# Value products of a head with its high and low columns in one stationary operand, in an encoder trunk on one core

## The chip, the cores and the metric

The kernel runs on one core of a Trainium2 chip. The metric is the device time of one execution in microseconds (us). It was run three times before the change: 2228.54, 2228.63 and 2228.89 us, median 2228.63.

## The reference

A trunk of two layers for 256 tokens of width 2048, in float32. Each layer norms its input, projects it to 4608 columns, and hands these to three groups: a gated convolution of width 31 with a layer norm, attention with 16 heads of 64, and a pooling group. Their results are normed, scaled, concatenated, projected back and added to the input; a gated feed-forward part of 5632 hidden columns follows. The attention mixes three dilated windows; for 256 tokens this comes to one softmax with a mask that adds a logarithm for keys seen by several windows:

```python
wgt = jnp.exp(m_all - jnp.max(m_all, axis=0, keepdims=True))
num = jnp.sum(wgt[..., None] * o_all, axis=0)
den = jnp.sum(wgt * s_all, axis=0)
out = num / den[..., None]
```

## The kernel before, in words

**Weights.** Every large product is x times a weight matrix, 512 output columns at a time (a `Job`). Activations and weights are split into a high and a low part of the type fp32r, and three products are summed: high x high, high x low, low x high (lines 139 to 141). A job is cut into groups of two blocks of 128 rows; a group is one DMA of 512 KB on SP's queue (line 90), a ScalarE copy that rounds to the high part (line 104) and a VectorE subtraction for the low part (line 113).

**Steps.** The order of the work is written out by hand. The main loop (line 876) goes through one group per step `s`: it first copies and splits the weights of the group three steps ahead (`pump`), then emits six matmuls for the first 128 tokens (`t` = 0) with the group of this step, then six for the other 128 tokens (`t` = 1) with the group four steps back, and last it calls `run_tasks`. When a job's last group is done for a `t`, its `done` function is called right behind the six matmuls. So a step is twelve matmuls and what the tasks add, and each engine works through its own instructions in this order. The tile framework adds the semaphores.

**Tasks.** A task is a generator. Each `yield n` means "go on n steps later" (1 without a number); `spawn(task, n)` starts it n steps later, and one that is due runs in the same call. Tasks run in the order of their start. `tr_free` (line 171) lets one of them per step take the tile for transposes; the transposes of q and k reserve theirs three steps after their projection.

**Attention.** The 16 heads are two halves of eight (called 0.0 to 0.7 and 1.0 to 1.7 in what follows; the code's names are `hf` and `h`). For each half q, k and v are projected in this order, two halves one after the other; each is a job of eight groups. In layer 0 the value projection of half 0 is done (`v_done`, line 521) at step 51 for `t` = 1, the one of half 1 at step 75, the k projection of half 1 at step 71. `v_last` starts the heads of half 0 one step later, every second step from 52 on; `k_last` (line 645) starts those of half 1 five steps after k, two in three steps, at 72, 73, 75, 76 and so on. The second layer has the same steps from its own start.

`head_task` (line 534) is one head: scores on TensorE (line 543, rows `r0` of 64, six matmuls), mask and maximum on VectorE (line 548), and the negated maximum on GpSimd; one step later the exponentials on ScalarE (line 556); one step later 1/denominator and normalisation on VectorE (lines 562 and 564); two steps later four transposes on TensorE (line 571), the high part on ScalarE (line 575) and the low part on VectorE (line 576); two steps later the value products (line 584). These take all 128 value columns of a pair of heads as stationary operand, so each head computes 64 rows that nobody reads: v high x p high, v high x p low, v low x p high for two blocks of keys, six in all, into `po[:, h % 2]`. `po` is one accumulator bank for the pair. After the odd head, in the same step, ScalarE scales the two row halves into the high part (line 600) and squares them (line 604), VectorE makes the low part (line 606), and GpSimd adds the squares (line 611). Two steps after the last pair `ssb` sums the squares over the rows (line 616) for the norm of the attention group.

Beside the first half's heads, the convolution runs on VectorE (line 383, three or four operations a step to step 57), then its layer norm (lines 395 to 412, with three operations of 512 columns per `t` at steps 61 and 65), and the transposes for the output product. From step 72 the output projection runs; its finished chunks are copied by ScalarE (`ac_done`, line 678), for `t` = 0 at steps 75, 79, 83 and 87 and for `t` = 1 four steps later.

**Buffers.** `s2` has six buffers of 512 columns for `pt` (the probabilities), `pT` (two per head), `sq` and others. `trp` has two accumulator banks, `scp` (scores) and `pop` (value results) one each.

Of the kernel before, what the change touches and what calls it, by code (L numbers as in the profile page):

```python
# [7 lines left out]
F32 = mybir.dt.float32  # L8
F32R = mybir.dt.float32r
AF = mybir.ActivationFunctionType  # L10
ALU = mybir.AluOpType
AX = mybir.AxisListType

P = 128
S = 256
NT = S // P
# [6 lines left out]
HD = 64  # L23
ROT = 16
NHH = HALF_B // HD
# [4 lines left out]
NB = 512  # L30
# [11 lines left out]
def hybrid_encoder_kernel(  # L42
# [6 lines left out]
    nc = tc.nc  # L49
# [4 lines left out]
    s4 = ctx.enter_context(tc.tile_pool(name="s4", bufs=23))  # L54
    s2 = ctx.enter_context(tc.tile_pool(name="s2", bufs=6))
# [96 lines left out]
    def spawn(gen, delay=0):  # L152
        tasks.append([clock["step"] + delay, gen])
# [17 lines left out]
    def tr_free():  # L171

        k = clock["step"]
        if used.get(k):
            return False
        used[k] = True
        return True
# [59 lines left out]
    rs_in = {}  # L237
# [82 lines left out]
    def mixer_jobs(l):  # L320
        st = {}
# [199 lines left out]
        def v_done(hf):  # L521
            def done(t, ps):
                if t == 0:
                    st["v", hf] = [
                        s4.tile([P, NT, NB], F32R, tag="s4", name="v") for _ in range(2)
                    ]
                hi, lo = (a[:, t] for a in st["v", hf])
                nc.scalar.activation(hi, ps, AF.Copy, scale=rs_in[t])
                nc.vector.scalar_tensor_tensor(
                    lo, ps, rs_in[t], hi.bitcast(F32), ALU.mult, ALU.subtract  # L530
                )
            return done

        def head_task(hf, h):
            qT, kT, v = st["qT", hf], st["kT", hf], st["v", hf]
            pr, r0 = h // 2, (h % 2) * HD
            sc = scp.tile([P, NT, S], F32, tag="sc", name="sc")
            pt = s2.tile([P, NT, S], F32, tag="s2", name="pt")
            mx = sm.tile([P, NT], F32, tag="mx", name="mx")
            den = sm.tile([P, NT], F32, tag="den", name="den")  # L540
            for t in range(NT):
                for i, (a, b) in enumerate(((0, 0), (0, 1), (1, 0))):
                    nc.tensor.matmul(  # L543
                        sc[:, t], qT[a][r0 : r0 + HD, pr, t * P : (t + 1) * P],
                        kT[b][r0 : r0 + HD, pr], start=i == 0, stop=i == 2,
                    )
            for t in range(NT):
                nc.vector.tensor_tensor_reduce(
                    pt[:, t], sc[:, t], mask[:, (1 - t) * P : (1 - t) * P + S], 1.0, -3.0e38, ALU.add, ALU.max,
                    accum_out=mx[:, t : t + 1],  # L550
                )
            nmx = sm.tile([P, NT], F32, tag="nmx", name="nmx")
            nc.gpsimd.tensor_scalar(nmx, mx, -(HD ** -0.5), None, ALU.mult)
            yield
            for t in range(NT):
                nc.scalar.activation(
                    pt[:, t], pt[:, t], AF.Exp, bias=nmx[:, t : t + 1], scale=HD ** -0.5,
                    accum_out=den[:, t : t + 1],
                )
            yield  # L560
            rden = sm.tile([P, NT], F32, tag="rden", name="rden")
            nc.vector.reciprocal(rden, den)
            for t in range(NT):
                nc.vector.tensor_scalar(pt[:, t], pt[:, t], rden[:, t : t + 1], None, ALU.mult)
            yield 2
            while not tr_free():
                yield
            pst = trp.tile([P, NT, S], F32, tag="tr", name="tr")
            for kt in range(NT):
                for t in range(NT):  # L570
                    nc.tensor.transpose(  # L571
                        pst[:, kt, t * P : (t + 1) * P], pt[:, t, kt * P : (kt + 1) * P], ident
                    )
            pT = [s2.tile([P, NT, S], F32R, tag="s2", name="pT") for _ in range(2)]
            nc.scalar.activation(pT[0], pst, AF.Copy)
            nc.vector.tensor_tensor(pT[1], pst, pT[0].bitcast(F32), ALU.subtract)
            yield 2
            if h % 2 == 0:
                st["po", hf] = pop.tile([P, 2, S], F32, tag="po", name="po")
            po = st["po", hf]  # L580
            n = 0
            for kt in range(NT):
                for a, b in ((0, 0), (0, 1), (1, 0)):
                    nc.tensor.matmul(  # L584
                        po[:, h % 2], v[a][:, kt, pr * P : (pr + 1) * P], pT[b][:, kt],
                        start=n == 0, stop=n == 5,
                    )
                    n += 1
            if h % 2 == 0:
                return  # L590
            if pr == 0:
                yB[hf] = [s4.tile([P, 4, S], F32R, tag="s4", name="yB") for _ in range(2)]
            hi, lo = yB[hf]
            col = G_MX + l * KD + 4 + 4 * hf + pr
            sq = sq_acc
            if (hf, pr) != (0, 0):
                sq = s2.tile([P, S], F32, tag="s2", name="sq")
            rows = [slice(e * HD, (e + 1) * HD) for e in range(2)]
            for e, r in enumerate(rows):
                nc.scalar.activation(  # L600
                    hi[r, pr], po[r, e], AF.Copy, scale=gT[r, col : col + 1]
                )
            for e, r in enumerate(rows):
                nc.scalar.activation(sq[r], po[r, e], AF.Square)
            for e, r in enumerate(rows):
                nc.vector.scalar_tensor_tensor(
                    lo[r, pr], po[r, e], gT[r, col : col + 1], hi[r, pr].bitcast(F32),
                    ALU.mult, ALU.subtract,
                )
            if sq is not sq_acc:  # L610
                nc.gpsimd.tensor_tensor(sq_acc, sq_acc, sq, ALU.add)
            if hf == 1 and pr == 3:
                yield 2
                ssb = scp.tile([P, NT], F32, tag="sc", name="ssb")
                for t in range(NT):
                    nc.tensor.matmul(
                        ssb[:, t : t + 1], sq_acc[:, t * P : (t + 1) * P], ones,
                        start=True, stop=True,
                    )
                ms = sm.tile([P, NT], F32, tag="msb", name="msb")  # L620
                nc.vector.tensor_scalar(ms, ssb, 1.0 / C_B, EPS, ALU.mult, ALU.add)
                rs = sm.tile([P, NT], F32, tag="rsb", name="rsb")
                nc.gpsimd.tensor_tensor(
                    rs, ms, half_neg.to_broadcast([P, NT]), ALU.pow
                )
                for t in range(NT):
                    rs_b[t] = rs[:, t : t + 1]
# [3 lines left out]
        def attn_task(hf, pace):  # L631
            for h in range(NHH):
                spawn(head_task(hf, h))
                yield pace[h % len(pace)]
# [10 lines left out]
        def k_last(hf, pace):  # L645
            base = qk_done("k", hf)

            def done(t, ps):
                base(t, ps)
                if t == NT - 1:  # L650
                    spawn(attn_task(hf, pace), 5)
            return done

        kin = [(k, k) for k in range(KD)]
# [106 lines left out]
    for l in range(DEPTH):  # L761
        jobs, load_layer = mixer_jobs(l)
        a = len(groups)
        add_jobs(jobs)
        seg_info.append((a, len(groups), load_layer, (g_post_mix, l), G_FF + l * KD))
        a = len(groups)
# [31 lines left out]
    for n in range(4):  # L798
        for t in range(NT):
            load_x(t, n)  # L800
            g = 2 * n + t
# [4 lines left out]
    gT = cst.tile([P, NG], F32, name="gT")  # L806
# [9 lines left out]
    rows = {}  # L816
# [48 lines left out]
    col = None  # L865
    for si, (g0, g1, load_layer, post, pre) in enumerate(seg_info):
        n = g1 - g0
# [99 lines left out]
        col = pre  # L967
# [55 lines left out]
```

## Time and profile before

| | |
|---|---|
| Median of three runs | 2228.63 us |
| The profiled execution | 2228.57 us |
| Its span | 2226.8 us |
| TensorE matmul busy | 2208.8 us, 99% of the span, 9860 matmuls |
| VectorE busy | 1287.8 us, 58% |
| ScalarE busy | 1060.3 us, 48% |
| GpSimd busy | 127.9 us, 6% |
| DMA | 400.66 MB, mean 180 GB/s |

The span is the time from the first to the last instruction of the profiled execution; 1.8 us of the execution's time lie around it. In the rows below PE is TensorE (PEld its weight loads), DVE is VectorE, ACT is ScalarE, POOL is GpSimd and SP is SyncE; L584 is line 584 of the kernel, and `out<-in` are the tiles written and read. Matmuls are pipelined, so the time of one is longer than the interval between two. The granted TensorE clock is 1.00 of full speed in both attention stretches.

### The profile page before, as it was taken

Reading aid. Unit: us, or ns where it says so; the run is one execution under the profiler, and the core shown is the slowest. Engines: PE = TensorE matmul, PEld = TensorE weight load, DVE = VectorE, ACT = ScalarE, POOL = GpSimd, SP = SyncE. Lnnn points to the kernel's source line nnn. Section 1 sums busy time; section 2 is a strip of 40 time slices with the busy share of each in tenths; the row PEclk is TensorE's granted clock in tenths of the full one; section 3 lists DMA queues with packets and bytes.
Section 4 is the critical chain, followed back from the end, with each engine's and each line's share of the span. In section 5 each row is a group of like instructions: output and inputs, shape, how many; then the busy total and the mean of one; then the engine's idle time right before and its main releaser. Section 6 shows DMA issues by size and latency. Waiting matters only on the chain.

```text
span 2226.8 us, 26295 instructions
## 1 busy us (share of the span) xinstructions
PE 2208.8 (99%) x9860; PEld 1778.8 (80%) x9860; DVE 1287.8 (58%) x1735; ACT 1060.3 (48%) x1481; POOL 127.9 (6%) x163
## 2 busy tenths in 40 slices
PE   9999999999999999999999999999999999999998
PEld 6887887888888888888778788878888888888886
DVE  5798757455444444455567987574544444444544
ACT  6445756444444443444564566564444444434443
POOL 0001112000000000000210011120000000000002
PEclk9999999999999999999999999999999999999999
DMA  8654355555555655556565544555555555555553
GB/s 268 194 176 136 133 172 178 181 182 186 189 182 187 183 185 186 186 182 204 172 210 177 171 132 149 173 170 180 189 180 189 188 180 183 186 188 181 188 199 123
DMA packets 208608, 400.66 MB, mean 180 GB/s; under 512 B 12730, under 2 KB 16162, under 8 KB 208480
## 3 DMA queue, kind: packets, MB, share of 16 engines
q1 hardware_dynamic: 208448, 398.98, 55.7%
q8 instruction: 77, 1.26, 0.2%
q14 instruction: 51, 0.42, 0.1%
q10 hardware_dynamic: 32, 0.01, 0.0%
HBM read 396.84 MB, written 2.10 MB: 179 GB/s over the span
## 4 chain that ended last, share of the span: by engine, by line
PE 95%; DVE 2%; ACT 2%; issue 1%; DMA 0%; POOL 0%; SPq 0%; DVEq 0%; POOLq 0%; ACTq 0%
PE acc L139 30%; PE acc L140 30%; PE acc L141 30%; PE tr L208 1%; PE sc L543 1%; PE po L584 1%; DVE hl L113 1%; ACT xT L215 1%; PE tr L571 1%; DVE xT L218 0%; ACT junk L202 0%; DMA raw<-in_w_in_dram 0%; DVE x L292 0%; PE tr L512 0%; PE tr L445 0%
## 5 line engine op out<-in xcount | busy, mean ns | idle before, releaser
L113 DVE TENSOR_TENSOR hl<-raw,hl 128x1024 fp32r<-128x1024 f32 x736 | 905.0, 1231 | 767.5 <-ACT hl L104 766.1
L104 ACT ACTIVATE hl<-raw 128x1024 fp32r<-128x1024 f32 x735 | 776.4, 1059 | 761.6 <-PE acc L141 752.7
L139 PE MATMUL acc<-hl,xT 128*128 128x512 f32 x1984 | 796.2, 401 | 1.0 <-DVE hl L102 1.0
L140 PE MATMUL acc<-hl,xT 128*128 128x512 f32 x1984 | 786.7, 397 | 1.4 <-DVE hl L113 1.2
L141 PE MATMUL acc<-hl,xT 128*128 128x512 f32 x1984 | 786.6, 396 | 1.3 <-DVE xT L218 1.3
L141 PEld LDWEIGHTS acc<-hl,xT 128*128 128x128 f32 x1984 | 373.6, 188 | 93.1 <-DVE xT L218 2.6
L139 PEld LDWEIGHTS acc<-hl,xT 128*128 128x128 f32 x1984 | 373.7, 188 | 90.1 <-ACT xT L215 2.0
L140 PEld LDWEIGHTS acc<-hl,xT 128*128 128x128 f32 x1984 | 374.0, 189 | 89.4 <-DVE hl L113 3.3
L139 PE MATMUL acc<-hl,fT 128*128 128x512 f32 x704 | 280.1, 398 | 0.0
L141 PE MATMUL acc<-hl,fT 128*128 128x512 f32 x704 | 279.1, 396 | 0.0
L140 PE MATMUL acc<-hl,fT 128*128 128x512 f32 x704 | 279.0, 396 | 0.0
L141 PEld LDWEIGHTS acc<-hl,fT 128*128 128x128 f32 x704 | 132.6, 188 | 32.3
L140 PEld LDWEIGHTS acc<-hl,fT 128*128 128x128 f32 x704 | 132.7, 188 | 31.8
L139 PEld LDWEIGHTS acc<-hl,fT 128*128 128x128 f32 x704 | 132.6, 188 | 31.7
L272 POOL TENSOR_TENSOR out<-out,gain 128x512 f32<-128x512 f32 x20 | 25.8, 1297 | 1447.4 <-ACT junk L202 1447.4
L383 DVE SCALAR_TENSOR_TENSOR cacc<-hT,cwT,cacc 128x241 f32<-128x241 f32 (+14 forms) x240 | 98.8, 469 | 0.0
L210 ACT ACTIVATE fT<-tr 128x512 fp32r<-128x512 f32 x44 | 26.4, 599 | 96.1 <-PE tr L208 96.1
L211 DVE TENSOR_TENSOR fT<-tr,fT 128x512 fp32r<-128x512 f32 x44 | 30.4, 692 | 68.6 <-ACT fT L210 68.6
L710 ACT ACTIVATE sg<-acc,rsin 128x512 f32<-128x512 f32 x44 | 30.3, 689 | 45.6 <-PE acc L141 45.6
L202 ACT ACTIVATE junk<-out 128x512 bf16<-128x512 f32 x32 | 20.2, 631 | 66.6 <-DVE out L740 42.8
L139 PE MATMUL acc<-hl,yB 128*128 128x512 f32 x128 | 51.1, 399 | 0.0
L140 PE MATMUL acc<-hl,yB 128*128 128x512 f32 x128 | 50.7, 396 | 0.0
(150 smaller groups left out, 1294.5 us busy)
## 6 DMA issues: line engine op xcount, KB each, us to landing
raw<-in_w_gate_dram SPq DMA_DIRECT2D x176, 512.0 KB, 3.5
raw<-in_w_up_dram SPq DMA_DIRECT2D x176, 512.0 KB, 3.5
raw<-in_w_down_dram SPq DMA_DIRECT2D x176, 512.0 KB, 3.6
raw<-in_w_in_dram SPq DMA_DIRECT2D x144, 512.0 KB, 3.6
raw<-in_w_out_dram SPq DMA_DIRECT2D x64, 512.0 KB, 3.5
x<-in_x_dram SPq DMA_DIRECT2D x8, 256.0 KB, 6.9
pm<-in_c_pool_dram SPq DMA_DIRECT2D x4, 512.0 KB, 5.2
gain<-in_g_post_mix_dram SPq DMA_DIRECT2D x4, 512.0 KB, 6.7
```

Source lines behind the costliest of these rows:

```text
L104: nc.scalar.activation(hl[:, 0], raw, AF.Copy)
L113: nc.vector.tensor_tensor(hl[:, 1], raw, hl[:, 0].bitcast(F32), ALU.subtract)
L139: nc.tensor.matmul(ps, xh, hl[:, 0, j], start=first, stop=False)
L140: nc.tensor.matmul(ps, xh, hl[:, 1, j], start=False, stop=False)
L141: nc.tensor.matmul(ps, xl, hl[:, 0, j], start=False, stop=last)
L208: nc.tensor.transpose(pst[:, j], srcs[j], ident)
L210: nc.scalar.activation(dst[:, 0], pst, AF.Copy)
L211: nc.vector.tensor_tensor(dst[:, 1], pst, dst[:, 0].bitcast(F32), ALU.subtract)
L215: nc.scalar.activation(dst[:, 0, j], pst[:, j], AF.Copy, scale=g)
L272: nc.gpsimd.tensor_tensor(o, o, gain, ALU.mult)
L383: nc.vector.scalar_tensor_tensor(acc[:, c, lo:hi], src, w, acc[:, c, lo:hi], ALU.mult, ALU.add)
L710: nc.scalar.activation(sg[t], ps, AF.Silu, scale=rs_in[t])
```

## The change

The value tiles are laid out anew: one tile per block of keys, in which each head has 128 columns, its 64 high and its 64 low columns side by side (for odd heads the low ones first). One stationary operand then holds both, and a head needs two products per block of keys, with the high and with the low part of the probabilities: four, not six. The result has the high part's rows in one half of the partitions and the low part's in the other; the low x low product is now part of the sum. One step later ScalarE copies the second half of the rows to the partitions of the first, and VectorE adds the two, into the `pt` tile of the even head (`yv`). For odd heads the scaled high part, the squares and the low part follow another step later, from `yv`, with all 128 rows at once, and the squares lie in `yv` too, except for the first pair. The value split of a projection is done in two pieces, for the even and the odd heads. The gaps ahead of the transposes and ahead of the value products are one step, not two; the last sum of squares comes one step, not two, after the last split; and `k_last` starts the heads of half 1 four steps after k, not five.

```diff
@@ v_done @@
                     st["v", hf] = [
-                        s4.tile([P, NT, NB], F32R, tag="s4", name="v") for _ in range(2)
+                        s4.tile([P, NHH, 2, HD], F32R, tag="s4", name="v") for _ in range(NT)
                     ]
-                hi, lo = (a[:, t] for a in st["v", hf])
-                nc.scalar.activation(hi, ps, AF.Copy, scale=rs_in[t])
-                nc.vector.scalar_tensor_tensor(
-                    lo, ps, rs_in[t], hi.bitcast(F32), ALU.mult, ALU.subtract
-                )
+                v = st["v", hf][t].rearrange("p (g e) c d -> p g e c d", e=2)
+                pv = ps.rearrange("p (g e d) -> p g e d", e=2, d=HD)
+                for e in range(2):
+                    hi, lo = v[:, :, e, e], v[:, :, e, 1 - e]
+                    nc.scalar.activation(hi, pv[:, :, e], AF.Copy, scale=rs_in[t])
+                    nc.vector.scalar_tensor_tensor(
+                        lo, pv[:, :, e], rs_in[t], hi.bitcast(F32), ALU.mult, ALU.subtract
+                    )
@@ head_task @@
+            gap = 1
...
-            yield 2
+            yield gap
             while not tr_free():
                 yield
...
-            yield 2
+            yield gap
             if h % 2 == 0:
                 st["po", hf] = pop.tile([P, 2, S], F32, tag="po", name="po")
-            po = st["po", hf]
+            po = st["po", hf][:, h % 2]
             n = 0
             for kt in range(NT):
-                for a, b in ((0, 0), (0, 1), (1, 0)):
+                vv = v[kt][:, h].rearrange("p c d -> p (c d)")
+                for b in range(2):
                     nc.tensor.matmul(
-                        po[:, h % 2], v[a][:, kt, pr * P : (pr + 1) * P], pT[b][:, kt],
-                        start=n == 0, stop=n == 5,
+                        po, vv, pT[b][:, kt], start=n == 0, stop=n == 3,
                     )
                     n += 1
+            yield
+            e = h % 2
+            r, r2 = slice(e * HD, (e + 1) * HD), slice((1 - e) * HD, (2 - e) * HD)
+            if e == 0:
+                st["yv", hf] = pt
+            yv = st["yv", hf]
+            nc.scalar.activation(yv[r, 1], po[r2], AF.Copy)
+            nc.vector.tensor_tensor(yv[r, 0], po[r], yv[r, 1], ALU.add)
             if h % 2 == 0:
                 return
+            yield
...
-                sq = s2.tile([P, S], F32, tag="s2", name="sq")
...
+                sq = yv[:, 1]
+            y, g = yv[:, 0], gT[:, col : col + 1]
+            nc.scalar.activation(hi[:, pr], y, AF.Copy, scale=g)
+            nc.scalar.activation(sq, y, AF.Square)
+            nc.vector.scalar_tensor_tensor(
+                lo[:, pr], y, g, hi[:, pr].bitcast(F32), ALU.mult, ALU.subtract
+            )
...
             if hf == 1 and pr == 3:
-                yield 2
+                yield
@@ k_last @@
-                    spawn(attn_task(hf, pace), 5)
+                    spawn(attn_task(hf, pace), 4)
```

## Rows read from the trace of the kernel before

**Rows 1.** The page: busy time by engine, and the chain that ended last.
```profile
PE 2208.8 (99%) x9860; PEld 1778.8 (80%) x9860; DVE 1287.8 (58%) x1735; ACT 1060.3 (48%) x1481; POOL 127.9 (6%) x163
...
PE 95%; DVE 2%; ACT 2%; issue 1%; DMA 0%; POOL 0%; SPq 0%; DVEq 0%; POOLq 0%; ACTq 0%
```

**Rows 2.** Groups by line: operation, shapes, count | busy us, mean ns | idle before, releaser.
```profile
L584 PE MATMUL po<-pT,v 128*128 128x256 f32 x192 | 28.4, 284 | 0.8 <-DVE yB L606 0.8
```

**Rows 3.** Timeline, TensorE, at step 61: start us, us, engine line op, count.
```profile
198.98 0.88 PE L584 MATMUL po<-pT,v 128*128 128x256 f32 x6
...
199.69 0.39 PE L139 MATMUL acc<-hl,xT 128*128 128x512 f32 x1
...
199.92 0.39 PE L140 MATMUL acc<-hl,xT 128*128 128x512 f32 x1
```

**Rows 4.** Waits of the whole run: who for whom, us in total, times, longest.
```profile
DVE yB L606 <- ACT sq L604: 28.7, 12, 3.6
...
PEld sc L543 <- DVE mx L548: 0.8, 2, 0.4
```

**Rows 5.** Windows over both layers' attention: busy us and count by engine, clock, DMA.
```profile
165.41:310.00 144.59, 144.06 (x740) 118.14 (x740) 110.22 (x252) 96.61 (x193) 22.17 (x31) 1.00 0.45 146
1270.00:1414.60 144.60, 144.08 (x741) 118.13 (x741) 110.19 (x252) 96.69 (x193) 22.25 (x31) 1.00 0.45 146
```

**Rows 6.** Groups by line: the row halves of a pair, and the addition of squares.
```profile
L606 DVE SCALAR_TENSOR_TENSOR yB<-po,gT,yB 64x256 fp32r<-64x256 f32 x32 | 15.5, 483 | 28.9 <-ACT sq L604 28.7
L600 ACT ACTIVATE yB<-po,gT 64x256 fp32r<-64x256 f32 x32 | 15.0, 468 | 26.5 <-PE po L584 26.1
...
L604 ACT ACTIVATE sq<-po 64x256 f32<-64x256 f32 x28 | 10.6, 378 | 0.4
L611 POOL TENSOR_TENSOR sq_acc<-sq_acc,sq 128x256 f32<-128x256 f32 x14 | 10.5, 747 | 84.1 <-ACT sq L604 84.1
```

**Rows 7.** Timeline, TensorE and VectorE, steps 54 to 56.
```profile
172.12 0.97 PE L543 MATMUL sc<-kT,qT 64*128 64x256 f32 x6
...
175.62 0.62 DVE L564 TENSOR_SCALAR pt<-pt,rden 128x256 f32<-128x256 f32 x2
...
178.75 0.60 PE L571 MATMUL tr<-ident,pt 128*128 128x128 f32 x4
...
180.41 1.22 DVE L113 TENSOR_TENSOR hl<-raw,hl 128x1024 fp32r<-128x1024 f32 x1
```

**Rows 8.** Timeline, step 75: behind the value projection's last matmul.
```profile
254.29 0.87 PE L584 MATMUL po<-pT,v 128*128 128x256 f32 x6
254.49 0.69 ACT L528 ACTIVATE v<-acc,rsin 128x512 fp32r<-128x512 f32 x1 [0.81 <-PE acc L141]
...
255.21 0.75 DVE L529 SCALAR_TENSOR_TENSOR v<-acc,rsin,v 128x512 fp32r<-128x512 f32 x1 [1.93 <-ACT v L528]
```

**Rows 9.** Timeline, TensorE and VectorE, end of step 65 and step 66.
```profile
219.41 0.60 PE L512 MATMUL tr<-ident,k 128*128 128x128 f32 x4
...
220.04 0.68 DVE L576 TENSOR_TENSOR pT<-tr,pT 128x512 fp32r<-128x512 f32 x1
```

**Rows 10.** Timeline, step 79: behind an output chunk's last matmul.
```profile
271.30 0.88 PE L584 MATMUL po<-pT,v 128*128 128x256 f32 x6
...
271.50 0.60 ACT L682 ACTIVATE out<-acc 128x512 f32<-128x512 f32 x1 [0.81 <-PE acc L141]
```

**Rows 11.** Timeline, TensorE and ScalarE, from step 82's transposes to step 83's.
```profile
284.94 0.60 PE L571 MATMUL tr<-ident,pt 128*128 128x128 f32 x4
...
286.89 0.60 ACT L575 ACTIVATE pT<-tr 128x512 fp32r<-128x512 f32 x1
...
287.52 0.51 ACT L556 ACTIVATE pt<-pt,nmx 128x256 f32<-128x256 f32 x1
...
288.52 1.04 ACT L104 ACTIVATE hl<-raw 128x1024 fp32r<-128x1024 f32 x1
...
289.28 0.60 PE L571 MATMUL tr<-ident,pt 128*128 128x128 f32 x4
```

More of the change, by code (lines that the diff above doesn't have):

```diff
@@ L596, in head_task @@
             if (hf, pr) != (0, 0):
-                sq = s2.tile([P, S], F32, tag="s2", name="sq")
[L598 to L609, printed above, removed]
+                sq = yv[:, 1]
[5 more added lines that the diff above has]
+            )
             if sq is not sq_acc:
```

## The prediction, made before the change was run

> **What bounds the kernel now.** Read the page first: TensorE is busy for 99% of the span, and the chain that ended last is 95% TensorE [rows 1]. So each product removed shortens the run by its issue interval, and each time TensorE has to wait lengthens it by the wait. Next, the lines by form: the value products are 192 matmuls [rows 2]. Their 284 ns is a latency; matmuls overlap. Ahead of them TensorE idled 0.8 us in all, for the VectorE split of the pair before. The interval is in the timeline: from a group of six to the next group's start 0.71 us, 0.12 us each [rows 3]. Then the waits: TensorE's weight loads for score products idled twice, 0.4 us each, for VectorE [rows 4]. Little else in attention stops TensorE. The two layers' attention stretches are equal to 0.1% and VectorE is busy for 76% of each [rows 5], so every term below is worked out in layer 0 and doubled.
>
> **What is removed.** Two of six value products per head, 32 heads: 64 x 0.12 = 7.7 us. The score waits (0.8 us) go, since the waits below leave VectorE time; the 0.8 us ahead of value products I leave standing, because the next head's product now comes right behind the same VectorE stretch. Gain: 8.5 us.
>
> **What costs nothing on its own.** Per pair, ScalarE ran two 468 ns and two 378 ns pieces; it will run two copies (at most 468) and two full-height pieces of the same length, whose time goes by columns: no more than before. VectorE ran two of 483 ns; it will run two sums and one split, three of at most 483 [rows 6], 0.5 us more per pair, inside its 24% idle time. If that cover were gone, 16 x 0.5 = 8 us. GpSimd keeps its one addition per pair (0.75 us). The loop issues DMAs and splits weights ahead of the tasks, in the same steps as before, so no DMA passes another on SP's queue. The last sum of squares moves from step 90 to 88, with a whole step between GpSimd's addition and TensorE: no wait.
>
> **What the shorter gaps cost.** Before, the transposes stand two steps behind the normalisation and the value products two steps behind the transposes; after, one. A step without attention is twelve weight matmuls, 2.86 us: from the score group at 172.12 less its 0.90 to the transposes at 178.75 are two of them [rows 7]. Everything TensorE waits for must get through the ScalarE and VectorE queues in that time.
>
> *Half 0, head 0.* The transposes move to step 55, which TensorE reaches at 172.12 + 0.90 + 2.86 = 175.9. Normalisation ends at 175.62 + 0.62 = 176.24 [rows 7]. The value split at step 51 also becomes copy, subtract, copy, subtract, each waiting for the one before: two subtracts of 0.48 with a copy of 0.47 between for one of 0.75 [rows 6, 8], 0.8 us later for all of VectorE. So the transposes wait until 177.1: 1.2 us. The low half of the transposed weights now stands behind step 55's four convolution operations, which end where 180.41 starts [rows 7]; with 0.8 of shift and 0.69 of its own it is ready at 181.9. TensorE gets to the products at 177.1 + 0.5 + 2.9 = 180.5: 1.4 us. Sum 2.6, or 1.75 without the shift. I take 2.5.
>
> *Half 0, head 4.* Its products come at the front of step 66, where TensorE now starts the k transposes at 219.41. The low half it needs is what VectorE does at 220.04, behind the three operations on the convolution's result, ready at 220.75 [rows 9]: 1.4 us even if nothing is added. The sum and the split of the pair before go into VectorE's queue ahead of it, and their ScalarE parts delay its weight split: at most 1.0 more. I take 1.9.
>
> *Half 1, head 0.* The spawn after 4 steps instead of 5, with both gaps halved, brings these products from step 78 to 75, right behind the last matmul of the value projection they read. There ScalarE starts the value copy at 254.49, with TensorE ready at 254.29 [rows 8]. Two products (0.24) use the first row block; the rest need copy 0.47, subtract 0.48 and two hand-overs of 0.05: 255.54. Wait 1.0; 2.1 if they wait for both halves of the columns.
>
> *Half 1, odd heads.* In this half the heads of a pair start one step apart, so the copy and sum of an even head stand in the same step as the odd head's products, just ahead of them, and read the other half of the same accumulator bank. VectorE's present split sits idle 28.7 us for ScalarE's squares, whose result it does not use [rows 4]: both only read that bank, so accesses of one bank are put in order. If this holds for products too, the odd head waits for the sum. At step 79 ScalarE first copies a finished output chunk, 271.50 to 272.10; then copy 0.38, sum 0.48, hand-overs 0.1: 273.0, against products at 271.30 [rows 10]: 1.7 us. In the other three pairs the sum is the end of a chain that starts where the transposes of the step before do: transposes 0.6, copy 0.6, exponentials 1.0, weight copy 1.04, weight split 1.22, sum 0.48, 4.9 us, while TensorE goes from transposes to the next step in 4.34 [rows 7, 11]: about 0.5 each, 0.7 for the first, where the value split is in the queue as well. Together 3.4.
>
> The Trainium skill ("PSUM — Partial Sum Buffer", section "PSUM bank collisions raise a hardware error") says that two engines on the same bank and the same 32 partitions must be kept apart, reads against reads and disjoint columns included. The rows show it for two readers; no row here shows it for a product's write against a reader. By the rule the 3.4 stand; by the rows alone they could be nothing.
>
> **Sum.** Per layer 2.5 + 1.9 + 1.0 + 3.4 = 8.8, both 17.6, less 8.5: +9.1 us. The profiled execution took 2228.57 (span 2226.8), 0.06 under the median. Forecast 2237.7 us.
>
> **Rivals.**
> *The queues keep up, faster.* VectorE's 28.7 us of idling for the squares go, because the new split reads no accumulator; if that brings the sums and low halves forward so far that they are ready within 2.86 us, the waits vanish and the gain is left: 2228.57 - 8.5 = 2220.1. Decides at 4.25 us of waits per layer. For: 14.3 us per layer is more than all waits. Against: head 0 comes before any split, head 4's delay is made by the convolution's operations, and the value copy of half 1 can't come earlier than its matmul. 0.12.
> *Columns, not banks, order the accumulator, no change.* The 3.4 go: +2.3, 2230.9. For: no row shows a write against a reader. Against: the squares. 0.20.
> *Scratch buffers, slower still.* The even head's probabilities tile stays in use until GpSimd's addition (0.75 us); if the next transposed copy gets that buffer, ScalarE waits for GpSimd in half 1 and the sum is later by 0.9 at step 76; with the value wait at 2.1: +2.0 per layer, 2241.7. The first products of a step can be hit too. Six buffers, all in use at step 75, speak for it; that the tile for the squares is no longer needed speaks against. 0.15.
> *The removal does not pay.* The interval of a product could be set by something other than its count, so that four take what six did: no 7.7, 2245.4. Against: 0.12 us per 256 columns is half the 0.23 per 512 of the weight matmuls around it [rows 3]. 0.03.
>
> **How the numbers follow.** The forecast has 0.50. About 0.2% (4.5 us) is what a measurement of this kernel can tell from no change. Faster by more: 0.12. Within: the second rival and 0.02 of the forecast's own, 0.22. Slower: 0.48 + 0.15 + 0.03 = 0.66. Lower bounds of the terms (1.75 + 1.4 + 1.0 + 0) twice, less 8.5: 2228.4. Upper (2.6 + 2.4 + 2.1 + 3.4 + 0.9) twice, less 8.5: 2242.9. The range 2228.4 to 2243 leaves out the first and last rival, 0.15 to 0.2.
>
> **What would show it.** Value products x128 with four in 0.48 us; in the waits view TensorE idling before them in both layers, about four times on VectorE's sum, once on its value subtract and about twice on its low halves; four waits of the odd heads in half 1, longest at step 79. A waits view with under 8.5 us of TensorE idling in attention makes the forecast wrong in sign; no wait on the sums makes the fourth term wrong.

## The result, and the profile after

The changed kernel takes 2250.30 us, the median of four runs (2249.91 to 2251.16); the kernel before took 2228.76 beside it. The ratio is 1.0097, with an interval of 1.0079 to 1.0114: 21.5 us slower. The forecast was 9.1 us slower and its range ended at 2243. The profiled execution took 2250.31 us with a span of 2248.5.

The page after (busy time by engine, and the chain that ended last), against [rows 1]:

```profile
PE 2212.4 (98%) x9796; PEld 1774.2 (79%) x9796; DVE 1296.0 (58%) x1759; ACT 1057.9 (47%) x1489; POOL 130.2 (6%) x163
...
PE 85%; DVE 9%; ACT 3%; issue 2%; POOL 0%; DMA 0%; SPq 0%; DVEq 0%; POOLq 0%; ACTq 0%
```

64 matmuls are gone, yet the busy time rose, and VectorE's share of the chain went from 2% to 9%. The groups by line say where (form, count | busy us, mean ns of one | idle before and its releasers); the first answers to [rows 2], the others to [rows 6]:

```profile
L589 PE MATMUL po<-pT,v 128*128 128x256 f32 x128 | 24.5, 302 | 16.5 <-DVE pT L580 8.6 <-DVE pt L600 5.9 <-DVE v L532 1.7
...
L600 DVE TENSOR_TENSOR pt<-po,pt 64x256 f32<-64x256 f32 x32 | 13.4, 419 | 7.8 <-ACT pt L599 7.4
L618 POOL TENSOR_TENSOR sq_acc<-sq_acc,pt 128x256 f32<-128x256 f32 x14 | 12.8, 914 | 50.4 <-ACT pt L613 50.4
L599 ACT ACTIVATE pt<-po 64x256 f32<-64x256 f32 x32 | 12.1, 379 | 2.2 <-PE po L589 1.3
L614 DVE SCALAR_TENSOR_TENSOR yB<-pt,gT,yB 128x256 fp32r<-128x256 f32 x16 | 10.6, 662 | 3.0 <-ACT yB L612 3.0
...
L531 ACT ACTIVATE v<-acc,rsin 128x256 fp32r<-128x256 f32 x16 | 7.6, 473 | 21.7 <-DVE v L532 16.7 <-PE acc L141 5.0
```

TensorE idles 16.5 us ahead of value products (0.8 before): for the low half of the transposed weights (L580), for the sums that read the accumulator (L600), and for the value split (L532). Three further things were not so before: the new low part L614 takes 662 ns, the one GpSimd addition per pair 914 ns instead of about 750, and ScalarE idles 16.7 us between the two pieces of a value split.

The timeline of TensorE in layer 0 (start us, us, line, tiles, count, idle before and releaser) shows the large waits one by one:

```profile
178.25 0.72 PE L575 MATMUL tr<-ident,pt 128*128 128x128 f32 x4 [1.52 <-DVE pt L568]
...
183.28 0.63 PE L589 MATMUL po<-pT,v 128*128 128x256 f32 x3 [1.39 <-DVE pT L580]
...
226.69 0.62 PE L589 MATMUL po<-pT,v 128*128 128x256 f32 x3 [2.65 <-DVE pT L580]
...
265.54 0.51 PE L589 MATMUL po<-pT,v 128*128 128x256 f32 x2 [0.85 <-DVE v L532]
...
285.00 0.74 PE L589 MATMUL po<-pT,v 128*128 128x256 f32 x4 [1.53 <-DVE pt L600]
```

A wait costs the time by which an interval between two starts exceeds its usual length (0.234 us behind a weight matmul, 0.12 behind a value product). By that measure, in layer 0: transposes of head 0.0 1.7, its products 1.55, head 0.4 2.8, head 0.6 1.0 in two parts, head 1.0 1.0, and the odd heads of half 1 0.5, 1.7, 0.5 and 0.6. Together 11.3 us, where the prediction had 8.8. The waits view of the whole run has the same waits twice, once per layer.

One thing has no place in the prediction. Windows of the changed kernel (us; busy and count of PE, PEld, DVE, ACT, POOL; granted TensorE clock; DMA share; GB/s), the first two in layer 0 around the wait of head 0.4, the others in the same place of layer 1:

```profile
226.00:229.00 3.00, 2.31 (x14) 2.01 (x15) 1.77 (x3) 2.97 (x6) 0.00 (x0) 0.94 0.29 98
229.00:233.00 4.00, 4.00 (x12) 3.09 (x12) 3.20 (x9) 1.53 (x4) 1.92 (x3) 0.62 0.37 126
...
1340.00:1344.00 4.00, 2.96 (x13) 2.57 (x13) 2.16 (x4) 3.97 (x8) 0.39 (x2) 0.67 0.41 135
1344.00:1349.00 5.00, 5.00 (x16) 3.78 (x15) 3.16 (x9) 0.87 (x1) 1.53 (x2) 0.58 0.31 106
```

Behind the 2.65 us wait the clock falls to its lower level (1.2 of 2.4 GHz) for a part of each window. The missing share of the clock times the window is 0.2 + 1.5 = 1.7 us in layer 0 and 1.3 + 2.1 = 3.4 in layer 1, 5.1 us. In [rows 5] the clock stood at 1.00 throughout.

The account: waits 2 x 11.3 = 22.6, clock 5.1, 64 products fewer -7.7: +20.0 of the 21.7 between the two profiled executions. Of the other 1.7, 0.6 is there at 15 us, ahead of any attention; the rest lies in intervals that are longer by less than 0.4 us each, which were not followed.

### The profile page after: what moved, and what is told of

Same layout as the page of the kernel before. It is cut to its first block, busy times and chain, and to the rows that moved or that the text cites. A ratio compares the mean times of both kernels' runs of the same rounds, so it can differ in the third digit from the quotient of the medians.

```text
span 2248.5 us, 26198 instructions
## 1 busy us (share of the span) xinstructions
PE 2212.4 (98%) x9796; PEld 1774.2 (79%) x9796; DVE 1296.0 (58%) x1759; ACT 1057.9 (47%) x1489; POOL 130.2 (6%) x163
## 4 chain that ended last, share of the span: by engine, by line
PE 85%; DVE 9%; ACT 3%; issue 2%; POOL 0%; DMA 0%; SPq 0%; DVEq 0%; POOLq 0%; ACTq 0%
PE acc L139 27%; PE acc L140 27%; PE acc L141 27%; DVE hl L113 3%; DVE cacc L383 3%; PE tr L208 1%; ACT hl L104 1%; PE sc L547 1%; PE po L589 1%; ACT xT L215 1%; ACT pt L560 1%; ACT junk L202 0%; DVE xT L218 0%; PE tr L575 0%; DVE x L292 0%
```

## The experiments

Diffs are against the changed kernel unless said otherwise. Positions are compared by the starts of the same weight matmul in two traces.

### What the gaps do alone, and the products alone

**The kernel before with the three shorter gaps and nothing else.**

```diff
@@ head_task, ahead of the transposes and again ahead of the products @@
-            yield 2
+            yield 1
@@ k_last @@
-                    spawn(attn_task(hf, pace), 5)
+                    spawn(attn_task(hf, pace), 4)
```

> The kernel before with nothing but the three shorter gaps: one step, not two, ahead of the transposes and ahead of the value products, and the heads of half 1 four steps after k. Six products, whole-tile value split, readers of the accumulator in the odd head's step as before. Theory (the gaps make the waits, the added copies, sums and the divided value split lengthen them): per layer the transposes of head 0.0 wait 0.35, its products 1.4, those of head 0.4 1.4, head 1.0 1.0, no waits of the odd heads of half 1; 4.2 per layer, 8.4 in all, so about 2237, and up to 5 more if the clock falls behind a wait as in the changed kernel. Rival (the gaps alone make the waits as long as they are in the changed kernel: 1.7, 1.5, 2.8, 1.0 and 1.0 for head 0.6): 8 per layer, 16 in all, so 2245, and 2250 with the clock; the wait of head 0.4 would be 2.8.

2249.75 us (2247.59 to 2250.84), ratio 1.0091 [1.0075, 1.0108]: 20.6 us slower, nearly as much as the whole change. The theory's 2237 is refuted. The rival had the time, but not the places: head 0.4 waits 1.0, not 2.8. The timeline of TensorE in this kernel:

```profile
181.49 0.85 PE L584 MATMUL po<-pT,v 128*128 128x256 f32 x5 [1.40 <-DVE pT L576]
...
225.12 0.86 PE L584 MATMUL po<-pT,v 128*128 128x256 f32 x5 [0.83 <-DVE pT L576]
...
242.51 0.86 PE L584 MATMUL po<-pT,v 128*128 128x256 f32 x5 [1.02 <-DVE pT L576]
...
274.63 0.72 PE L571 MATMUL tr<-ident,pt 128*128 128x128 f32 x4 [0.70 <-DVE pt L564]
```

The products of heads 0.0 (1.55) and 1.0 (1.0 in two parts) wait about as worked out; the transposes of head 0.0 don't wait. What the theory did not have: head 0.6 waits 1.8 (0.5 and 1.3, the second at 242.51), and in half 1 four transposes wait 0.8 to 0.9 each (one at 274.63). VectorE's timeline says why the latter:

```profile
272.93 0.98 DVE L606 SCALAR_TENSOR_TENSOR yB<-po,gT,yB 64x256 fp32r<-64x256 f32 x2 [2.55 <-ACT sq L604]
```

The normalisation stands behind the split that idles for ScalarE's squares [rows 4]; with one step instead of two that idling reaches TensorE. The changed kernel has no such wait, since its split reads no accumulator. By the measure used above the waits come to 8.7 per layer. In the profiled execution the clock fell once, behind the wait at 181.49 in layer 0, and nowhere in layer 1's attention; layer 0's attention ends 11.5 us late, layer 1 adds 9.5. The 2.0 between them is close to the 1.7 that the clock's windows give (0.2 of 181 to 184, 1.5 of 184 to 188).

**The kernel before without its last value product.** Diff against before; value low x probabilities high is left out, nothing else differs.

```diff
-                for a, b in ((0, 0), (0, 1), (1, 0)):
+                for a, b in ((0, 0), (0, 1)):
...
-                        start=n == 0, stop=n == 5,
+                        start=n == 0, stop=n == 3,
```

> The kernel before, with the product of the low value columns and the high probabilities left out (that part of the result is missing): four products per head, and nothing else changed. Theory (0.12 us for each product): -7.7 us, 2221.0. Rival (the products' time is set by something other than their count): less than 2 us.

2222.84 us, ratio 0.9972 [0.9961, 0.9983]: 6.0 us faster. The weight matmuls come about 0.24 us earlier behind nearly every head, two products of 0.12 us, as [rows 3] said; 0.25 is given back twice, at the wait for the split that was left standing. So the removal pays: 6.0 of the 7.7 predicted, and 0.5 of the rest is that wait.

**Four products with the old gaps.** Copies, sums and split stand in the odd head's step, in a tile of their own; the value split is one piece, as in a later experiment, and the other two steps are as before.

```diff
-            gap = 1
+            gap = 2
...
-            yield
-            e = h % 2
...
             if h % 2 == 0:
                 return
-            yield
+            yv = s2.tile([P, 2, S], F32, tag="s2", name="yv")
+            for e in range(2):
+                r, r2 = slice(e * HD, (e + 1) * HD), slice((1 - e) * HD, (2 - e) * HD)
+                nc.scalar.activation(yv[r, 1], st["po", hf][r2, e], AF.Copy)
+                nc.vector.tensor_tensor(yv[r, 0], st["po", hf][r, e], yv[r, 1], ALU.add)
```

> Four products with high and low columns side by side, but the gaps and the start of the kernel before; the copies, sums and split of a pair in the odd head's own step, in a tile of their own; the value split in one piece. Theory (the products are free to go, the cost lies in the shorter gaps and in reading the bank between two heads): 2221 us, at most 1 us of waits in attention. Rival (the sums are more than VectorE can take: 0.5 us per pair and 8 us in all): 2228 or more.

2230.82 us, ratio 1.0009 [1.0000, 1.0018]. With the long gaps, the value split in one piece and the readers of a pair together, 19.5 us of the changed kernel's time are gone, but the products' 7.7 don't show: new waits use them up. TensorE's waits in layer 0:

```profile
PE sc L546 <- DVE mx L551: 1.8, 2, 0.9
PE po L588 <- DVE yv L598: 1.2, 1, 1.2
PE tr L512 <- DVE yTA L218: 1.1, 1, 1.1
PE tr L208 <- DVE yTC L218: 0.4, 1, 0.4
```

ScalarE's timeline:

```profile
242.70 0.38 ACT L597 ACTIVATE yv<-po 64x256 f32<-64x256 f32 x1
244.68 0.38 ACT L597 ACTIVATE yv<-po 64x256 f32<-64x256 f32 x1 [1.59 <-DVE yv L598]
245.55 0.51 ACT L607 ACTIVATE yB<-yv,gT 128x256 fp32r<-128x256 f32 x1 [0.49 <-DVE yv L598]
```

Copy, sum, copy, sum on one bank lets neither engine go ahead of the other: ScalarE idles 2.1 us in this pair. That TensorE's waits come from this order is not shown by this run; the two versions at the end, which change only when these operations come, show how much of them does.

### One wait at a time

**Copies and sums of both heads one step behind the odd head, in half 1 alone.**

```diff
-            yield
             e = h % 2
...
             if e == 0:
                 st["yv", hf] = pt
+                if hf == 1:
+                    return
+            yield
...
+            for e in range(e if hf == 0 else 0, e + 1):
```

> The changed kernel, with the copies and sums of a pair together behind the odd head in half 1 alone; half 0 as changed. Theory (the four waits of odd heads in half 1 come from readers of the same bank, and what the joint copies cost came from half 0): 3.3 to 3.5 us less in each layer, 2243.5 us. Rival (VectorE is late with everything, waits only move): 2248 or more.

2244.74 us, ratio 1.0072 [1.0058, 1.0086]; 6.6 us less than the changed kernel at the last weight matmul, 3.3 per layer. The waits of TensorE in layer 0 (what waits <- for what: us in all, times, longest), first the sums' line of the changed kernel, then all of this one:

```profile
PE po L589 <- DVE pt L600: 2.9, 5, 1.5
...
PE po L589 <- DVE pT L580: 4.3, 3, 2.6
PE tr L575 <- DVE pt L568: 1.5, 1, 1.5
PE po L589 <- DVE v L532: 0.8, 1, 0.8
PE po L589 <- DVE pt L603: 0.3, 1, 0.3
```

Of the five waits for sums four are gone, and the one left (0.3) is in half 0. With the readers out of the odd head's way nothing comes in their place: a product that writes one half of a bank does wait for a sum that reads the other half. That is the order that the Trainium skill asks for ("PSUM — Partial Sum Buffer", section "PSUM bank collisions raise a hardware error"), and the trace agrees. The bank is one tile of the program here, so the runs don't tell whether the order goes by bank or by tile.

**The same in both halves.**

```diff
-            yield
-            e = h % 2
...
             if h % 2 == 0:
+                st["yv", hf] = pt
                 return
             yield
+            yv = st["yv", hf]
+            for e in range(2):
...
+                nc.scalar.activation(yv[r, 1], st["po", hf][r2, e], AF.Copy)
+                nc.vector.tensor_tensor(yv[r, 0], st["po", hf][r, e], yv[r, 1], ALU.add)
+            yield
```

> The changed kernel, but the copies and sums of both heads of a pair stand together one step behind the odd head, so that nothing reads the accumulator bank between the two heads' products. Theory (the odd heads of half 1 wait for a reader of the other columns of the same bank): the four waits of half 1, 0.5, 1.7, 0.5 and 0.6 us in each layer, go: -6.6 us, 2243.7. Rival (the odd heads wait because VectorE is late with everything, and would wait for the low half of their own weights anyway): less than 2 us.

2247.72 us (2247.51 to 2252.44), ratio 1.0089 [1.0074, 1.0104]. In the profiled execution half 1 gains 3.2 per layer, and half 0 loses 2.9 in layer 1 and 6.1 in layer 0, where the clock takes 3.4 more than in the changed kernel. The longest new wait is that of a head's transposes for the pooling group's transposed copies on VectorE:

```profile
224.20 0.66 PE L575 MATMUL tr<-ident,pt 128*128 128x128 f32 x4 [1.29 <-DVE yTC L218]
```

The execution with the profile, 2252.44, had a mean clock of 0.995, the three others, at 2247.5 to 2247.8, 0.997 to 0.998. A clock lower by 0.0025 is 5.6 us of 2250, so it accounts for the 5 us between them.

**High columns first for all heads, so the value split is one copy and one subtraction.**

```diff
-                for e in range(2):
-                    hi, lo = v[:, :, e, e], v[:, :, e, 1 - e]
-                    nc.scalar.activation(hi, pv[:, :, e], AF.Copy, scale=rs_in[t])
...
+                hi, lo = v[:, :, 0], v[:, :, 1]
+                pv = ps.rearrange("p (h d) -> p h d", d=HD)
+                nc.scalar.activation(hi, pv, AF.Copy, scale=rs_in[t])
```

> The changed kernel, with every head's high columns first, so that the value split is one copy and one subtract again. Theory (alternating pieces hold ScalarE up for VectorE, and this delays half 0's head 0 by about 1.3 us per layer; the wait at head 1.0 grows by 0.3 since a whole copy and a whole subtract stand ahead): -2 us, 2248.3. Rival (the shift of VectorE is made up for elsewhere and head 0 is late for the convolution alone): +0.6 us, 2250.9.

2249.43 us, ratio 1.0093 [1.0078, 1.0108]. The wait of head 0.0's transposes is gone, 1.7 per layer, so it was the divided value split that made it; head 1.0 waits 1.5 instead of 1.0, since its copy and subtraction now go over all the columns. But a fall of the clock now follows the products of head 0.0, 1.7 us in layer 0, and the time is the same.

**Half 1 one step later.** `spawn(attn_task(hf, pace), 4)` becomes 5.

> The changed kernel with one part undone: the heads of half 1 start five steps after k, not four. Theory (the 21.5 us are separate waits of TensorE, each for its own late operand, plus the half clock behind the longest): only the wait of head 1.0 for its value split goes, 1.0 us in each layer, 2248.3 us. Rival (VectorE as a whole has become too slow, so a wait that is removed turns up at the next operand): no more than 0.5 us, 2249.8 to 2250.3.

2249.89 us, ratio 1.0096 [1.0080, 1.0113]. The wait of head 1.0 is gone, 1.0 per layer, but the odd heads, a step later than before, wait 0.8, 0.75, 1.7 and 0.6 instead of 0.5, 1.7, 0.5 and 0.6. Half of the gain is given back, and the other half, 0.9 in all, doesn't stand out from the spread of the runs.

**Two steps ahead of the products of head 0.4 alone.**

```diff
-            yield gap
+            yield 2 if (hf, h) == (0, 4) else gap
```

> The changed kernel with one gap restored for one head: the products of head 0.4 two steps behind its transposes. Theory (the 2.8 us wait at step 66 pulls the clock down behind it): the wait goes, 5.6 us for both layers, and the two stretches at half clock (3.4 and 6.8 us) with it, another 5.1: 2239.6 us, no half clock before the end of the run. Rival (the clock falls for the sum of idle time in attention, not for this wait): -5.6, with the clock still falling, 2244.7; or the wait moves to head 0.5: no change.

2252.90 us, ratio 1.0108 [1.0093, 1.0123]. The wait at step 66 is gone, but head 0.4's sum falls into the step of head 0.5's products:

```profile
239.92 1.22 PE L589 MATMUL po<-pT,v 128*128 128x256 f32 x4 [4.80 <-DVE pt L600]
```

The same bank again, and the sum stands behind the convolution's transposed copies in VectorE's queue: 5.0 us for 2.8.

**Two steps ahead of the products in all of half 0**: `yield gap` there becomes `yield 2 - hf`.

> The changed kernel with two steps again between transposes and products in half 0 alone. Theory: the waits of heads 0.0, 0.3, 0.4 and 0.6 for the low half of their weights go (about 1.5, 0.6, 2.9 and 0.5 us per layer), and the half clock with them (5.1 us): about -16 us, 2234. Rival (VectorE as a whole is too slow): the waits come back at the transposes or at half 1, -5 us or less.

2245.76 us, ratio 1.0074 [1.0057, 1.0091]. The waits for low halves are gone; two waits for sums come (1.8 us, and 2.8 at head 1.0, which takes the bank over from head 0.7), and the clock falls behind the second in both layers:

```profile
234.41 0.74 PE L589 MATMUL po<-pT,v 128*128 128x256 f32 x4 [1.68 <-DVE pt L600]
...
261.05 0.71 PE L589 MATMUL po<-pT,v 128*128 128x256 f32 x4 [2.66 <-DVE pt L600]
```

**The convolution's normalisation for the second 128 tokens one step later**, out of head 0.4's way: `yield` ahead of it becomes `yield 1 + t`.

> The changed kernel, with the three VectorE operations of the convolution's norm for the second 128 tokens moved from step 65 to step 66, so that they stand behind the low half that head 0.4's products wait for. Theory (head 0.4's wait of 2.9 us is these three operations ahead of the low half): -5.6 us for the waits of both layers and up to 5 for the half clock behind them, 2240 to 2245. Rival (head 0.4 is late for the sum of VectorE's work since step 52): the wait stays within 0.5 us, 2249 to 2251.

2262.65 us, ratio 1.0147 [1.0132, 1.0163]. Head 0.4 waits 0.6 instead of 2.8, so the three operations of the normalisation were what it waited for. But the heads behind it wait 2.9 and 3.1 us:

```profile
234.73 1.73 PE L589 MATMUL po<-pT,v 128*128 128x256 f32 x4 [2.71 <-ACT pT L579]
...
245.17 1.19 PE L589 MATMUL po<-pT,v 128*128 128x256 f32 x4 [2.94 <-DVE pt L600]
```

In the profiled execution the clock falls behind both, twice 3.4 us per layer, and the kernel is 12 us slower than the changed one.

Two steps ahead of the transposes of half 0, with the rest as changed, was not run.

### A version that is faster than both

**Old gaps, and both copies ahead of both sums** (diff against the four products with the old gaps):

```diff
-            for e in range(2):
...
+            for e, r in enumerate(halves):
+                nc.scalar.activation(yv[r, 1], st["po", hf][halves[1 - e], e], AF.Copy)
+            for e, r in enumerate(halves):
                 nc.vector.tensor_tensor(yv[r, 0], st["po", hf][r, e], yv[r, 1], ALU.add)
```

> Four products with the gaps of the kernel before, everything in the odd head's step, but both ScalarE copies ahead of both VectorE sums (alternating, ScalarE waited 1.6 us for a sum and VectorE 0.4 for the second copy). Theory (the alternation made VectorE late): half of the 4.3 us of waits that the alternating version had in layer 0 go, 2225 to 2228. Rival (the sums themselves are too much for VectorE): 2230 or more.

2227.32 us, ratio 0.9993 [0.9984, 1.0002]: 3.5 us less than the alternating order. In attention ScalarE's largest idling behind VectorE, in the groups by line, is ahead of the scaled high part:

```profile
L608 ACT ACTIVATE yB<-yv,gT 128x256 fp32r<-128x256 f32 x16 | 8.2, 510 | 22.1 <-DVE yv L599 22.1
```

**And the scaled high part, squares and low part one step later** (diff against the last; the sum of squares still comes two steps behind the last sums):

```diff
                 nc.vector.tensor_tensor(yv[r, 0], st["po", hf][r, e], yv[r, 1], ALU.add)
+            yield
...
             if hf == 1 and pr == 3:
-                yield 2
+                yield
```

> As the one with both copies first, but the scaled high part, the squares and the low part one step later, from the sums in SBUF, so that VectorE does not wait for ScalarE between sum and low part. Theory (the products' gain is there once VectorE is not held up): 2222 to 2225. Rival: the same as the version with both copies first, or slower, since the extra VectorE work is what counts.

2221.93 us (2221.49 to 2222.00), ratio 0.9968 [0.9955, 0.9980]: 7.0 us faster than before, 28 faster than the changed kernel. The same group now:

```profile
L609 ACT ACTIVATE yB<-yv,gT 128x256 fp32r<-128x256 f32 x16 | 8.0, 501 | 1.2 <-DVE yv L599 1.1
```

and all of TensorE's waits in layer 0's attention:

```profile
PE po L588 <- DVE yv L599: 0.7, 1, 0.7
```

The weight matmuls come 0.24 us earlier behind nearly every head and 6.9 earlier at the end; the clock does not fall before the end of the run. So with the long gaps, the value split in one piece, the copies first and the row split a step later, the new layout gives what the removed products are worth.

## Why the prediction was wrong in its size

**What it had right.** The direction; the removal (0.24 us per head); what waits, and for what, in five of the six places. Head 1.0: 1.0 predicted, 1.0 measured. Odd heads of half 1: 0.7 + 1.7 + 0.5 + 0.5 = 3.4 predicted; 0.5 + 1.7 + 0.5 + 0.6 = 3.3 measured, and the experiment in half 1 showed their cause. Head 0.0: 2.5 predicted, 3.2 measured; with the value split in one piece it is 1.55, so the divided split, taken at 0.8, cost 1.7.

**Half 0, head 4** was taken at 1.9, with "at most 1.0 more" than 1.4; it was 2.8. VectorE's timeline of the changed kernel at steps 64 and 65:

```profile
220.32 1.00 DVE L614 SCALAR_TENSOR_TENSOR yB<-pt,gT,yB 128x256 fp32r<-128x256 f32 x1
...
223.78 0.80 DVE L407 TENSOR_SCALAR yA<-tr,mv,rstd 128x512 f32<-128x512 f32 x1
224.62 0.69 DVE L411 TENSOR_TENSOR yA<-yA,lnp 128x512 f32<-128x512 f32 x1
225.35 0.69 DVE L412 TENSOR_TENSOR yA<-yA,lnp 128x512 f32<-128x512 f32 x1
225.96 0.68 DVE L580 TENSOR_TENSOR pT<-tr,pT 128x512 fp32r<-128x512 f32 x1
```

and GpSimd's:

```profile
220.30 0.73 POOL L618 TENSOR_TENSOR sq_acc<-sq_acc,pt 128x256 f32<-128x256 f32 x1
```

The order is as predicted, [rows 9] with the sum and the split ahead. But the split took 1.00 us, not 0.48, where GpSimd's addition had begun 0.02 earlier. With the gaps alone, where this split and sum are not in the way, head 0.4 waited 1.0: the change's own work added 1.8, where 0.5 was taken. VectorE is busy without a break from the weight split below to the low half in both kernels, first the changed one, then the gaps alone:

```profile
217.21 1.22 DVE L113 TENSOR_TENSOR hl<-raw,hl 128x1024 fp32r<-128x1024 f32 x1 [0.89 <-ACT hl L104]
...
216.67 1.23 DVE L113 TENSOR_TENSOR hl<-raw,hl 128x1024 fp32r<-128x1024 f32 x1 [0.35 <-ACT hl L104]
```

So the 1.8 is the split (1.0), a weight copy of ScalarE that comes 0.54 later, and TensorE, which is 0.24 earlier by two products.

**The sum** is the step that failed: "Per layer 2.5 + 1.9 + 1.0 + 3.4 = 8.8, both 17.6, less 8.5". It took its four places for all there are, and an us of waiting for an us of time. Of the 12.4 us between 9.1 and 21.5, the mis-sized terms are 2 x (0.7 + 0.9 - 0.1) = 3.0; head 0.6, which the prediction didn't look at, is 2 x 1.0 = 2.0; the clock behind the wait of head 0.4 is 5.1. The other 2.3 stay unassigned: in the profiled execution 0.6 of them lie ahead of attention, the others among the intervals that are longer by less than 0.4 us each. The clock is the largest single part, and no upper bound of the range held it. That the terms stood as a sum of independent ones failed too: three of the experiments that took away a wait (half 1 later, head 0.4 later, the normalisation later) moved it to the next late operand, the first at half its price and the others at more than all of it, and only the bank order in half 1 came away clean. Of the gaps themselves the prediction had four waits in three heads; alone they cost 20.6 us, with waits at head 0.6 and at the transposes of half 1 that it had nowhere.

**What costs nothing on its own** held for the count of operations and failed for their order. VectorE has the idle time, but two engines that take turns spend it in waiting: with the old gaps, 3.5 us for the alternating copies and sums and 5.4 for the split in the same step.

**The rivals.** That the queues keep up, and that columns order the accumulator, are refuted by the result and by the experiment in half 1. The scratch buffers did not take part: no row of the waits view has an engine waiting for GpSimd's addition. That the removal does not pay is refuted by the kernel with four products.

## What to carry to other kernels

Where one engine is busy for 99%, a gap between stages is slack that every operation in the other queues draws on: before shortening it, list what each operand waits behind in every step, not only at the places that the change names. Readers of one accumulator bank on two engines belong together, one engine's reads first, and away from the products that write the bank's other half; where they stand still has to be looked up in the queues, since the same order gained in half 1 and lost in half 0. And give the clock a place in the upper bound: where a wait of a microsecond or more is forecast, a fall behind it cost 1.7 or 3.4 us here.

## What the hardware showed that was not expected

TensorE's clock, at 1.00 through both attention stretches before, fell to its lower level behind single waits in a stretch that is otherwise busy: behind one of 2.65 us in the changed kernel, behind one of 1.40 with the gaps alone, and not behind the 1.39 at 183.28 in the changed kernel. One fall cost 1.7 or 3.4 us. What decides which wait is followed by one stays open; the mean clock differs from one execution of a kernel to the next, and the time with it, by up to 5 us.

A VectorE operation slowed by GpSimd: of the 16 splits L614 (two inputs in SBUF) the six that began behind GpSimd's addition, by 0.02 to 0.71 us, took 0.96 to 1.00 us, the other ten 0.45 to 0.48. At 278.63 VectorE began first:

```profile
278.63 0.48 DVE L614 SCALAR_TENSOR_TENSOR yB<-pt,gT,yB 128x256 fp32r<-128x256 f32 x1
```

and GpSimd's addition was the longer one, 0.95 us for the 0.73 at 220.30:

```profile
278.75 0.95 POOL L618 TENSOR_TENSOR sq_acc<-sq_acc,pt 128x256 f32<-128x256 f32 x1
```

The old split [rows 6], which read the accumulator, took 0.48 us in the mean and GpSimd's addition 0.75. The Trainium skill ("SBUF — State Buffer", section "SBUF: two separate sides") says that a VectorE operation with two SBUF inputs and a GpSimd operation that reads SBUF take the same ports by turns, each for the whole instruction, whichever starts first. The rows agree on which of the two is slowed; the split lost about 0.5 us, less than the addition's 0.73.
